# A depthwise convolution on TensorE: eight time phases by sixteen channels in place of four by thirty-two, in a tuned transformer layer

## The chip, the cores and the metric

One Trainium2 chip, all 8 cores. Time is the device time of the slowest core in microseconds (us). The batch has 4 sequences of 4096 tokens; two cores share a sequence. The even cores compute 2176 tokens (two token groups, 1152 and 1024), the odd ones 1920 (768 and 1152) and a halo of 512 tokens of context in front. Nothing is exchanged between cores. In some runs the cores of one die, or of both, show a lower granted clock and the time is 1364 to 1602 us, with most of the kernels here; those runs are set aside and only fast runs are compared. "Even" and "odd" below are the mean span of the four even or odd cores over the fast runs of one kernel.

## The reference, cut to what matters

```python
x = x + 0.5 * swiglu(rmsnorm(x), ...)            # FFN 1
z = rmsnorm(x) @ w_in                            # q, k, v, and u = (a | b) for the convolution
attn_out = chunk_band_attention(q, k, v, bias)   # 8 heads of 64, 576 keys per 64 queries
g  = a * sigmoid(b)                              # GLU, 512 channels
dw = depthwise_causal_conv(g, width=31) + dw_bias
conv_out = silu(layernorm(dw) * ln_g + ln_b)     # norm over the 512 channels
x = x + concat(attn_out, conv_out) @ w_out
x = x + 0.5 * swiglu(rmsnorm(x), ...)            # FFN 2
y = rmsnorm(x)
```

## The kernel before

Each core runs FFN 1, the projections, the convolution, attention, the output projection and FFN 2 on its first token group, and then all of this on the second. From the first down product of FFN 2 of the first group (the matmuls `ps<-at,ring`) to the end of FFN 1 of the second is one long stretch of 393 us, mostly TensorE.

The convolution is done as matmuls. GLU results g[channel, time] go out to DRAM and come back (the "gather") in a phase layout: partition = 32 x phase + channel of the group, column = time / 4. In that layout one matmul against an expanded diagonal matrix of 128 x 128 takes 4 output phases from 4 input phases, and 9 column shifts cover the 31 taps. There are 16 groups of 32 channels:

```python
for s4 in range(4):                         # to_phases(): only after both channel halves are written
    src = d_[:, :, s4, :]
    dst = gp[32 * s4:32 * s4 + 32, :, u0:u0 + W]
    P.dma("sp", ..., reads=(("gs", gi, 0), ("gs", gi, 1)), ...)
...
for grp in range(16):                       # conv()
    for d in range(9):
        mm(b, 0, wv[:, grp % 2, d, :], gp[:, grp, 8 - d:8 - d + U], U, d == 0, d == 8, ...)
    dve(... tensor_scalar(out=acc[:, grp], in0=bank, scalar1=bias, op0=add))     # evacuation
    act(gp[:, grp, 0:U], acc[:, grp], AF.Square, ...)
    if grp > 0:
        pool(... sums += acc[:, grp])
...
for q in range(4):                          # conv_ln(): f32 all the way
    dve(a = a - mean);  dve(a = a * rstd)
for grp in range(16):
    act(co[:, grp, 0:U], acc[:, grp, 0:U], AF.Silu, U, ..., bias=bcol, scale=gcol)
```

U is a quarter of the tokens: 288 and 256 columns on even cores. The kernel places the instructions of all engines in one order by a model of their durations (`P.est`, `P.t`); filler work, the V and Q projections, goes where TensorE would wait by that model. Where the model still expects TensorE to wait for 0.8 us or more, the kernel issues placeholder matmuls (`keep_warm()`, the rows `ps<-cb_sb` of 128x256 at L545), whose results nobody reads. The order is fixed when the kernel is built.

The softmax here doesn't subtract the row's maximum and nothing guards it: scores larger than these inputs give would overflow.

Of the kernel before, what the change touches and what calls it, by code (L numbers as in the profile page):

```python
# [7 lines left out]
F32 = mybir.dt.float32  # L8
# [14 lines left out]
UMAX = MMAX // 4  # L23
GW = UMAX + 8
VW = 520
# [10 lines left out]
CS_LNG = 48  # L36
CS_LNB = 64
CS_RB = 80
CS_N = 84
# [3 lines left out]
CB_I32 = CB_ID + 256  # L43
CB_N = CB_I32 + 32
# [7 lines left out]
RING_COLS = 18832  # L52
# [194 lines left out]
class Group:  # L247


    def __init__(self, gi, blocks):  # L250
# [23 lines left out]
        self.U = self.M // 4  # L274

def build_nc(debug=None):
# [14 lines left out]
    cmp_d = din("cmp", [128, 576])  # L291
# [5 lines left out]
    with ExitStack() as es:  # L297
# [11 lines left out]
        gh_t = sb("gh", 16 * 8 * 2, BF16)[:, :].rearrange("p (g u) -> p g u", g=16)  # L309
# [9 lines left out]
        cmp_t = pb_f[:, 0:576]  # L319
        i32_t = pb_f[:, 576:608]  # L320
# [14 lines left out]
        O_GP = O_ACC + 64 * UMAX  # L335
        O_AB = O_GP + 32 * GW
        O_MV = O_AB + 8 * UMAX
        O_P = O_MV + 8 * UMAX
        O_RS = O_P + 4096
        assert O_RS + 4096 <= D_BYTES  # L340
        O_CV = O_ACC + 32 * UMAX
        qT = carve(O_Q, 8 * MMAX, BF16).rearrange("p (j t) -> p j t", j=4)
        acc = carve(O_ACC, 64 * UMAX, F32).rearrange("p (g u) -> p g u", g=16)
        cvt = carve(O_CV, 8 * MMAX, BF16).rearrange("p (c t) -> p c t", c=4)
        gp = carve(O_GP, 32 * GW, BF16).rearrange("p (g u) -> p g u", g=16)
        co = carve(O_GP, 32 * UMAX, BF16).rearrange("p (g u) -> p g u", g=16)
        sums = carve(O_AB, 4 * UMAX, F32).rearrange("p (i u) -> p i u", i=1)
        mv = carve(O_MV, 8 * UMAX, F32).rearrange("p (i u) -> p i u", i=2)
        mvb = carve(O_MV, 8 * UMAX, BF16).rearrange("p (i u) -> p i u", i=2)
# [18 lines left out]
        cwb = carve(O_GP, 9216, BF16).rearrange("p (i c) -> p i c", i=2)  # L368
# [14 lines left out]
        def make(half):  # L383
# [3 lines left out]
            gs_d = [nc.dram_tensor("gscr%d_%d" % (half, g.gi), [32, 16, 4, g.U + g.hist // 4], BF16).ap() for g in G]  # L387
            cr_d = [nc.dram_tensor("cscr%d_%d" % (half, g.gi), [32, 16, 4, g.U], BF16).ap() for g in G]
            cw_d = nc.dram_tensor("cwscr%d" % half, [8, 128, 2304], BF16).ap()
            gTs = [carve(O_ACC, 32 * (g.U + g.hist // 4), BF16).rearrange("p (c s u) -> p c s u", c=4, s=4) for g in G]  # L390
            c2s = [carve(O_ACC, 32 * g.U, BF16).rearrange("p (c s u) -> p c s u", c=4, s=4) for g in G]
# [39 lines left out]
            for g in G:  # L431
                W = g.U + g.hist // 4
                for c in range(4):
                    P.reg(("g", g.gi, c), "d", O_ACC + c * 8 * W, O_ACC + (c + 1) * 8 * W)
                    P.reg(("c2", g.gi, c), "d", O_ACC + c * 8 * g.U, O_ACC + (c + 1) * 8 * g.U)
            for i in range(16):
# [9 lines left out]
            P.reg("cmp", "pb", 0, 1152)  # L446
            P.reg("i32", "pb", 1152, 1216)
# [14 lines left out]
            P.reg("asum", "d", O_AB, O_AB + 4 * UMAX)  # L462
            P.reg("mean", "d", O_MV, O_MV + 4 * UMAX)
            P.reg("var", "d", O_MV + 4 * UMAX, O_MV + 8 * UMAX)
            P.reg("gph", "d", O_GP, O_GP + 16 * 2 * GW)
            for i in range(2):
                P.reg(("cwb", i), "d", O_GP + 4608 * i, O_GP + 4608 * (i + 1))
# [67 lines left out]
            def keep_warm(gap, skip):  # L535
# [4 lines left out]
                if b is None or P.est("pe", (), (("ps", b),)) > P.t["pe"] + 0.2:  # L540
                    return
                n = int((gap - 0.3) / (0.25 if P.t["pe"] < 9 else 0.125))
                o = bank(b)[:, 0:256]
                for i in range(n):
                    P.op("pe", lambda h: h.matmul(o, lhsT=onesS, rhs=cb[:, B_ONES:B_ONES + 256], start=True, stop=True,  # L545
# [27 lines left out]
            def pool(fn, n, reads, writes):  # L573
                P.op("pool", fn, 0.3 + n / 590.0, reads, writes)
# [457 lines left out]
            def to_phases(g, pc, u0, W):  # L1032
# [9 lines left out]
                if pc == 0:  # L1042
                    return
# [704 lines left out]
```

## Time and profile before

| | us |
|---|---|
| median of 6 runs | 1350.36 |
| even cores, odd cores (mean span, fast runs) | 1347.5 to 1347.9, 1339.4 to 1340.0 |
| core 6, first token group: start to first convolution matmul | 333.9 |
| from there to the first attention matmul | 35.3 |
| from there to the first down product of FFN 2 | 178.2 |
| the rest of FFN 2, and FFN 1 of the second group | 393.2 |
| from there to the first attention matmul of the second group | 75.8 |
| from there to the end | 319.3 |

I cut the run of core 6 into these stages, and asked for the busy time of each engine in each stage. Columns: stage, its length, then the busy time of TensorE (PE), weight loads, VectorE (DVE), ScalarE (ACT) and POOL, then clock, DMA share, GB/s.

```profile
333.90:369.20 35.30, 35.30 (x225) 22.61 (x225) 19.84 (x29) 14.09 (x28) 16.11 (x23) 0.95 0.72 156
369.20:547.40 178.20, 176.12 (x1546) 108.66 (x1546) 76.97 (x160) 89.56 (x149) 34.62 (x35) 1.00 0.40 85
547.40:940.60 393.20, 393.20 (x2075) 202.81 (x2074) 128.40 (x203) 85.47 (x150) 60.30 (x75) 1.00 0.45 85
940.60:1016.40 75.80, 74.20 (x425) 40.98 (x424) 34.97 (x56) 28.88 (x52) 22.72 (x33) 1.00 0.70 160
1016.40:1335.70 319.30, 311.78 (x2223) 168.75 (x2222) 114.93 (x218) 111.47 (x179) 41.32 (x52) 1.00 0.33 64
```

Length less PE busy is PE's idle time: 2.1 us in the first attention stage (which takes in the output projection and the first gate and up products of FFN 2), 7.5 us from the second attention to the end. The elementwise work of the convolution stands in the groups by shape (after the count: busy us, mean ns of one, then the engine's idle time before them and who ended it):

```profile
L1235 DVE TENSOR_SCALAR dreg<-ps,cs_sb 128x288 f32<-128x288 f32 x16 | 8.3, 518 | 14.9 <-PE ps L557 14.2 <-ACT dreg L567 0.7
...
L567 ACT ACTIVATE dreg<-dreg,cs_sb 128x288 bf16<-128x288 f32 x16 | 8.4, 611 | 0.0
L567 ACT ACTIVATE dreg<-dreg 128x512 bf16<-128x512 bf16 x9 | 6.0, 663 | 17.1 <-DVE dreg L1098 17.1
```

In this order: evacuation with the bias, the Silu, and the copy that puts GLU results in phase order. The f32 layernorm (L1277) takes 1358 ns for each of its products.

### The profile page before, as it was taken

Reading aid. Unit: us, or ns where it says so; the run is one execution under the profiler, and the core shown is the slowest. Engines: PE = TensorE matmul, PEld = TensorE weight load, DVE = VectorE, ACT = ScalarE, POOL = GpSimd, SP = SyncE. Lnnn points to the kernel's source line nnn. Section 1 sums busy time; section 2 is a strip of 40 time slices with the busy share of each in tenths; the row PEclk is TensorE's granted clock in tenths of the full one; section 3 lists DMA queues with packets and bytes.
Section 4 is the critical chain, followed back from the end, with each engine's and each line's share of the span. In section 5 each row is a group of like instructions: output and inputs, shape, how many; then the busy total and the mean of one; then the engine's idle time right before and its main releaser. Section 6 shows DMA issues by size and latency. Waiting matters only on the chain.

```text
span 1348.5 us, 22933 instructions; the slowest of 8 cores (1339.4 to 1348.5 us)
## 1 busy us (share of the span) xinstructions
PE 1312.1 (97%) x8454; PEld 736.6 (55%) x8454; DVE 489.0 (36%) x887; ACT 414.2 (31%) x722; POOL 251.6 (19%) x293
## 2 busy tenths in 40 slices
PE   8999999999999999999999999999999999999995
PEld 4565655565666655656555444444466564444444
DVE  4422222362655622222266222225346462122225
ACT  3310011352476531001246110113438661100123
POOL 2360000340402320000062000015140230000012
PEclk9999999999999999999999999999999999999997
DMA  9774226255741473342345744344673016532703
GB/s 220 157 189 80 49 53 115 37 114 132 154 83 23 97 170 63 50 91 51 59 64 104 209 78 85 61 86 85 160 162 85 3 34 124 91 66 45 127 1 127
DMA packets 34882, 127.56 MB, mean 95 GB/s; under 512 B 3408, under 2 KB 13776, under 8 KB 27856
## 3 DMA queue, kind: packets, MB, share of 16 engines
q0 software_dynamic: 18752, 96.10, 38.1%
q1 hardware_dynamic: 16016, 29.95, 7.3%
q8 instruction: 71, 1.16, 0.4%
q14 instruction: 43, 0.35, 0.1%
HBM read 191.98 MB, written 18.09 MB: 156 GB/s over the span
## 4 chain that ended last, share of the span: by engine, by line
PE 90%; DMA 4%; DVE 3%; issue 1%; ACT 1%; POOL 1%; SPq 0%; DVEq 0%; ACTq 0%; POOLq 0%
PE psA L557 52%; PE ps L557 38%; DMA ring<-wgu 2%; DVE hT L813 1%; DMA dreg<-gscr 1%; DMA gscr<-dreg 0%; DMA xres<-xin 0%; ACT rstd L567 0%; POOL xres L700 0%; DVE xres L996 0%; DVE dreg L1412 0%; ACT dreg L567 0%; ACT L565 0%; POOL ring L659 0%; DVE xres L1511 0%
## 5 line engine op out<-in xcount | busy, mean ns | idle before, releaser
L557 PE MATMUL psA<-hT,ring 128*128 128x512 bf16 (+2 forms) x3776 | 700.6, 347 | 5.5 <-DVE hT L813 2.4
L557 PEld LDWEIGHTS psA<-hT,ring 128*128 128x128 bf16 x3776 | 368.0, 98 | 331.7 <-issue 13.5
L567 ACT ACTIVATE dreg<-psA 128x512 f32<-128x512 f32 (+4 forms) x278 | 163.2, 592 | 670.3 <-PE psA L557 662.0
L557 PE MATMUL ps<-at,ring 128*128 128x512 bf16 (+2 forms) x1840 | 326.2, 339 | 0.0
L962 DVE TENSOR_TENSOR at<-psA,dreg 128x512 bf16<-128x512 f32 (+2 forms) x216 | 131.8, 611 | 452.6 <-PE psA L557 435.3
L557 PEld LDWEIGHTS ps<-at,ring 128*128 128x128 bf16 x1840 | 180.0, 98 | 144.4
L996 DVE SCALAR_TENSOR_TENSOR xres<-ps,xres 128x512 f32<-128x512 f32 (+2 forms) x152 | 87.4, 577 | 168.8 <-PE ps L557 168.8
L756 POOL TENSOR_TENSOR ssum<-ssum,sq 128x512 f32<-128x512 f32 (+2 forms) x100 | 104.8, 1049 | 213.2 <-ACT sq L567 210.1
L659 POOL DMA_DIRECT2D ring<-wgu x47 | 28.1, 603 | 476.6 <-PE psA L557 292.5
L557 PE MATMUL ps<-dreg,ring 128*128 128x256 bf16 (+3 forms) x672 | 99.8, 304 | 3.1 <-DMA dreg<-gscr 2.8
L567 ACT ACTIVATE sq<-xres 128x512 bf16<-128x512 f32 (+2 forms) x105 | 55.7, 536 | 105.2 <-DVE xres L996 67.9
L557 PEld LDWEIGHTS ps<-dreg,ring 128*128 128x128 bf16 x672 | 64.3, 99 | 28.6 <-issue 4.9
L813 DVE SCALAR_TENSOR_TENSOR hT<-xres,cs_sb,rstd 128x512 bf16<-128x512 f32 (+2 forms) x112 | 71.6, 696 | 15.0 <-ACT rstd L567 12.4
L557 PE MATMUL ps<-hT,ring 128*128 128x512 bf16 (+2 forms) x320 | 58.9, 339 | 0.0
L565 ACT ACT_TABLE_LOAD x38 | 48.8, 1283 | 0.7
L557 PEld LDWEIGHTS ps<-hT,ring 128*128 128x128 bf16 x320 | 30.9, 98 | 25.1 <-issue 0.2
L567 ACT ACTIVATE dreg<-dreg 128x288 bf16<-128x288 f32 (+6 forms) x53 | 25.4, 479 | 53.4 <-DVE dreg L1235 26.6
L567 ACT ACTIVATE pb<-psA 128x1024 bf16<-128x1024 f32 (+2 forms) x42 | 37.8, 914 | 4.5 <-PE psA L557 4.2
L1511 DVE TENSOR_TENSOR xres<-ps,xres 128x256 f32<-128x256 f32 (+2 forms) x48 | 25.2, 532 | 37.8 <-PE ps L557 37.8
L659 POOL DMA_DIRECT2D ring<-wdA x16 | 8.7, 544 | 131.4 <-PE psA L557 131.4
L1530 POOL TENSOR_TENSOR dreg<-pb 128x2304 bf16<-128x2304 bf16 x8 | 32.3, 4046 | 2.4 <-DMA cwscr<-dreg 2.4
L557 PE MATMUL ps<-at,hT 128*128 128x512 bf16 x136 | 30.7, 379 | 0.0
(89 smaller groups left out, 611.8 us busy)
## 6 DMA issues: line engine op xcount, KB each, us to landing
ring<-wgu POOLq DMA_DIRECT2D x41, 1024.0 KB, 10.0
ring<-wdA POOLq DMA_DIRECT2D x16, 768.0 KB, 8.4
ring<-wdB POOLq DMA_DIRECT2D x16, 640.0 KB, 7.2
ring<-cwscr POOLq DMA_DIRECT2D x16, 576.0 KB, 4.5
cwscr<-dreg SPq DMA_DIRECT2D x8, 576.0 KB, 4.5
ring<-wab POOLq DMA_DIRECT2D x8, 512.0 KB, 7.9
ring<-wout POOLq DMA_DIRECT2D x4, 1024.0 KB, 8.9
dreg<-xin SPq DMA_DIRECT2D x2, 2048.0 KB, 23.4
```

What stands on the lines that cost most here:

```text
L557: P.op("pe", lambda h: h.matmul(o, lhsT=lhsT, rhs=rhs, start=start, stop=stop, skip_group_check=True), (max(n / 2400.0 + 0.0025, 0.03) if ...
L565: P.op("act", lambda h: h.activation(out=cs[0:1, CS_N + i:CS_N + i + 1], in_=onesS[0:1, 0:1], func=func), 1.5, ("cb1",), ())
L567: P.op("act", lambda h: h.activation(out=out, in_=in_, func=func, **kw), 0.12 + n / 1200.0 + (0.09 * sum(isinstance(v, bass.AP) for v in k ...
L659: P.dma("pool", lambda h, dst=dst, src=src: h.dma_start(out=dst, in_=src), wtok(p, i), (256 if p.reads else 512) * w, reads=p.reads, after ...
L756: pool(lambda h: h.tensor_tensor(out=ss, in0=ss, in1=sqt, op=ALU.add), n, (sk, ("sq", i)), (sk,))
L813: dve(lambda h, dst=dst, xin=xin, gcol=gcol: h.scalar_tensor_tensor(out=dst, in0=xin, scalar=gcol, in1=rt, op0=ALU.mult, op1=ALU.mult), n, ...
L962: dve(lambda h: h.tensor_tensor(out=at, in0=ub, in1=tt, op=ALU.mult), n, (("ps", bU), ("tmpF", ti)), (("AT", gi, fl, s),))
L996: dve(lambda h, xo=xo, xi=xi, bk=bk: h.scalar_tensor_tensor(out=xo, in0=bk, scalar=0.5, in1=xi, op0=ALU.mult, op1=ALU.add), n, (("ps", b), ...
L1511: dve(lambda h, xo=xo, bk=bk: h.tensor_tensor(out=xo, in0=bk, in1=xo, op=ALU.add), n, (("ps", b),) + rk, (("x", gi, dm, s),))
L1530: P.op("pool", lambda h, o_=o_, i0=i0: h.tensor_tensor(out=o_, in0=i0, in1=i1, op=ALU.mult), 4.1, ("cmp", "i32", "cb"), (("cwb", i % 2),))
```

## The change

With 8 phases of 16 channels a matmul of half the columns does the same outputs per column, and 5 shifts instead of 9 cover the taps: 32 x 5 = 160 matmuls of an eighth of the tokens in place of 144 of a quarter. Around this the elementwise work is redone: several channel groups share a PSUM bank and are evacuated by one instruction; the gather is split by channel halves, so that the first half can come back while the second is computed; layernorm works in bf16 and takes gain and bias to VectorE; four long Silu replace sixteen. The model's figures for POOL and for the landing of the convolution weights are set higher. The core of the diff, cut:

```diff
-                if pc == 0:
-                    return
-                for s4 in range(4):
-                    src = d_[:, :, s4, :]
-                    dst = gp[32 * s4:32 * s4 + 32, :, u0:u0 + W]
-                    P.dma("sp", ..., reads=(("gs", gi, 0), ("gs", gi, 1)), ...)
-                hold["keys"] = (("gp", 0),)
+                lo, hi = pc * NG // 2, (pc + 1) * NG // 2
+                for s_ in range(PH):
+                    src = gs_d[gi][pc].rearrange("(h j) c s u -> h (j c) s u", h=CH)[:, :, s_, :]
+                    dst = gp[CH * s_:CH * s_ + CH, lo:hi, u0:u0 + W]
+                    P.dma("sp", ..., reads=(("gs", gi, pc),), ...)
+                if pc == 1:
+                    hold["keys"] = (("gp", lo),)
 ...
-                    for d in range(9):
-                        mm(b, 0, wv[:, grp % 2, d, :], gp[:, grp, 8 - d:8 - d + U], U, ...)
+                    for x, grp in enumerate(ids):            # several groups in one bank
+                        for d in range(ND):                  # ND = 5, NG = 32, PH = 8, CH = 16
+                            mm(b, x * U, wv[:, grp % per, d, :], gp[:, grp, HC - d:HC - d + U], U, ...)
+                    dve(... tensor_tensor(out=a3, in0=b3, in1=bc, op=add), m * U)   # one evacuation a bank
 ...
-                    dve(a = a - mean);  dve(a = a * rstd)                           # f32
-                for grp in range(16):
-                    act(co[:, grp], acc[:, grp], AF.Silu, U, bias=bcol, scale=gcol)
+                    dve(c_ = a - mean);  dve(c_ = c_ * rstd)                        # bf16 out
+                    for i in range(nq):                      # 8 groups a quarter, 32 in all
+                        dve(... tensor_scalar(x * gcol + bcol), U)
+                for q, (ck, c_) in enumerate(q_):
+                    act(c_, c_, AF.Silu, nq * U, ck, ck)                            # 4 long ones
 ...
-                P.op("pool", fn, 0.3 + n / 590.0, reads, writes)
+                P.op("pool", fn, 0.45 + n / 490.0, reads, writes)
```

## The prediction

> **What bounds the kernel now.** I read the page first, then the cores, the timeline of TensorE around the convolution, the sub-windows of its granted clock, and the timeline of the queue that issues the transposes.
>
> ```profile
> PE 1312.1 (97%) x8454; PEld 736.6 (55%) x8454; DVE 489.0 (36%) x887; ACT 414.2 (31%) x722; POOL 251.6 (19%) x293
> PE 90%; DMA 4%; DVE 3%; issue 1%; ACT 1%; POOL 1%; SPq 0%; DVEq 0%; ACTq 0%; POOLq 0%
> ```
>
> TensorE (PE) is busy for 97% of the span and is 90% of the chain that ended last. Elementwise time beside it costs nothing; matmul time removed should come off almost whole, and so should PE's waits. The even cores (2176 tokens) set the end at 1347 to 1348.5 us; the odd ones (1920 and a halo) end at 1339 to 1343, so a gain on even cores counts until they meet the odd ones.
>
> Next the convolution, in the timeline of PE: start, length, and in brackets the idle time before it.
>
> ```profile
> 333.88 19.52 PE L557 MATMUL ps<-dreg,ring 128*128 128x288 bf16 x144 [2.79 <-DMA dreg<-gscr]
> ...
> 333.88 6.37 PE L557 MATMUL ps<-dreg,ring 128*128 128x288 bf16 x37 [2.79 <-DMA dreg<-gscr]
> ...
> 988.27 15.94 PE L557 MATMUL ps<-dreg,ring 128*128 128x256 bf16 x144
> ```
>
> A length includes the drain of the last matmul, some 0.17 us. First token group: 144 matmuls of 288 columns. The first 37 took 6.2 us without the drain (168 ns each), the other 107 took 13.15 us (123 ns each). The second group's 144 of 256 columns took 15.8 us (109.6 ns each). The slow start is the clock:
>
> ```profile
> 334.00:337.00 3.00, 3.00 (x15) 1.89 (x14) 0.52 (x1) 0.28 (x1) 1.06 (x2) 0.56 0.36 90
> 337.00:340.00 3.00, 3.00 (x23) 2.27 (x22) 1.03 (x2) 0.81 (x3) 1.30 (x2) 0.87 0.78 303
> 340.00:343.00 3.00, 3.00 (x27) 2.40 (x25) 1.55 (x3) 1.13 (x3) 2.77 (x6) 1.00 0.65 204
> ```
>
> The third column from the right is the granted clock: 0.56 after the wait of 2.79 us, then 0.87, then 1.00. The wait thus cost 2.8 us, and 6.2 - 37 x 0.123 = 1.7 us more. The wait is for the gather of the phase layout out of DRAM; the chain of waits puts the two trips so:
>
> ```profile
> 317.98 5.41 DMA gscr<-dreg
> ...
> 325.64 8.00 DMA dreg<-gscr
> ```
>
> What narrow matmuls cost, each with its own weight load, the timeline of PE in attention shows:
>
> ```profile
> 382.01 0.42 PE L557 MATMUL ps<-at,dreg 128*128 128x65 bf16 x8
> ...
> 385.30 0.39 PE L557 MATMUL ps<-cb_sb,dreg 128*128 128x128 bf16 x4
> ```
>
> Less the last one's modelled length (194 and 218 ns in the groups by shape), seven steps of 65 columns are 0.226 us, 32 ns each, and three of 128 columns 0.172 us, 57 ns each. [...]
>
> [...] The gather of core 5's first group has runs of 400 B (200 positions of bf16) and took 8.5 us from its first issue, at 357.14, to PE's start at 365.65, the 576 B of core 6 took 10.0 us (323.61 to 333.64), and its 512 B in the second group 8.6; no penalty shows down to 400 B, and 288 B no run has shown. [...]
>
> **The change, part by part.** The depthwise convolution is done as matmuls against expanded diagonal matrices. Before: 4 time phases by 32 channels on the partitions, 16 channel groups, 9 shifts. After: 8 phases by 16 channels, 32 groups, 5 shifts; columns per matmul halve.
>
> 1. PE, convolution: group one 144 x 123 ns = 17.7 us becomes 32 x 5 = 160 of 144 columns [...]. Group two 15.8 us becomes 160 of 128 columns at 56 ns (the burst gave 57), 9.0 us: -6.8. Sum -14.5 us.
> 2. PE, statistics: 17 matmuls per group become 32 + 3 and 32 + 4 of half the width; [...]1.9 against 36 x 56 = 2.0. Sum +0.2 us.
> 3. The way to phases. Before, both channel halves must be written before four gathers of 2048 runs start. After, the first half is gathered (8 issues) while the second is computed; PE has about 12 us of gating matmuls between the two first writes (304.6 and 317.0). For the second half: one write (some 5 us), 8 issues at 0.62 us = 5.0 us against 2.6, and half the bytes: my estimate is 0.4 + 4.7 + 5.0 + 3 = 13 us where it was 16.6 (317.0 to 333.6). PE had its last K matmul at about 331.1, which is 14 us after. So the wait of 2.8 and the cold 1.7 us should mostly go: -4.5 us in full, of which I count three quarters, -3.4.
> 4. Convolution weights: pieces of 2560 columns for 2304. Those behind the K weights wait for the gather (as now: POOL issued three from 334.6 to 339.4), then for the first and second pieces to be released. PE now wants a piece each 1.25 us, and the last at 8.8 us after the start; the last can be issued some 3.5 us after the start and takes 4.5 us or more[...]. 0 to 2 us of wait, part of it filled by V projections: +1.
> 5. VectorE. PSUM evacuation: 16 of 518 ns = 8.3 us become 11 of up to 432 columns, at most 0.61 us (from 425 and 692 ns at 256 and 512): 6.5. Layernorm: eight of 1.36 us = 10.8 become four of 1.36 and four bf16 products of about 0.8, and the gain and bias leave ScalarE for 32 small ones of some 0.23 us = 7.5: about 16. Net some +3 us a group.
> 6. ScalarE: 16 Silu of 611 ns = 9.8 us become 4 of about 1.15 = 4.6; Squares 7.1 become about 6. Net -6 us a group. Both engines have slack (53.7 and 40.6 us busy in the 72 us of the first attention), so 5 and 6 matter only where PE waits for them: PE idles 1 us there and 3.1 us in the second. Count 0, with 1.5 us either way.
> 7. The way back: 16 writes of short runs for 8 and 2 large reads for 4: issue 10 us for 5, but it ends long before the output projection, under attention. 0.
> 8. Start: the tap table is 0.65 MB for 0.29 (128 x 1280 f32), but queued behind the first four weight pieces for which PE waits; five memsets go. +0.5.
> 9. The order of instructions is fixed by a model in the program, whose constants for POOL and DMA latency change. PE waits 4.7 us for POOL's sums of squares, mostly in tails without other work. -0.5.
>
> Sum: -14.5 + 0.2 - 3.4 + 1 + 0 + 0.5 - 0.5 = -16.7 on even cores. The order of the whole program shifts, and reordering seldom helps by chance: I give 1 us back, -15.7, so about 1334.7 us. On odd cores the first group has 192 columns (12.1 us for 144)[...]; they would end near 1331 and stay behind the even ones.
>
> **Rivals.**
> A. [...] For: the burst is short and the convolution is a long stream. Against: 32 ns at 65 columns, also in runs of 16. 15%.
> B. The wait for the gather stays or grows: 288 B runs cost as much as 512 B and 8 issues come one after the other. For: each 0.6 us issue is serial. Against: 400 B ran well, and half the work is done early. If it takes 18 us instead of 13, PE idles 4 us and goes cold: about 1340. 20%.
> C. PE becomes bound by DMA on the weights or by VectorE in the layernorm, so that attention starts late: 2 to 6 us lost, 1338 to 1341. Against: PE has V and Q projections to fill with. 20%.
> D. The better-known latencies also remove waits in the attention: 1 to 4 us more, 1331. 15%.
>
> **Range and chances.** 1334.7 us (-1.2%), 8 in 10 between 1329 and 1341. 2% would be 27 us, nearly twice all the matmul time that can go with both waits: faster by over 2% 0.03; slower by over 2% 0.01, as only an unforeseen stall could do it; within 2% 0.96.
>
> **What would show it.** 160 matmuls of 144 and of 128 columns in some 10 and 9 us[...], some 8523 matmuls in all, PE near 1298 us busy; the wait for the gather before the first group under 1 us and the clock at 1.00 behind it (rival B: above 3 us); waits for convolution weights under 2 us (C); VectorE some 6 us up and ScalarE some 12 us down without effect on the span. I am wrong if PE's busy time falls by 14 us and the span does not: then the idle time has moved, most likely to the start of attention.

Where the text is marked as cut, it spoke of the hardware without a trace or run of this case behind it, or rested on that. Three groups of numbers go with the cuts: in step 1 the term of the first group's matmuls, -7.7 us, as the time of a matmul of 144 columns came from there; in step 2 the first group's 0.1; and the odd cores' -5.3 and -7.7. The sum still counts them: -16.7 us on even cores, -15.7 and 1334.7 us with 1 given back, and -13 on odd ones. An estimate of that time from the traces alone, on a straight line between the 57 ns at 128 columns and the 109.6 at 256, is 63.6 ns, so 10.2 us for 160 and a term of -7.5. Rival A, its figures cut, says that narrow matmuls go more slowly in a long stream than in a burst of four. What was cut on the time of a weight load was not shown: the traces record 97 to 99 ns for one, overlapping the next, beside matmuls that follow each other at 32 and 57 ns.

Some other figures are estimates for which the prediction names no trace. An issue was put at 0.62 us, here and in the expectation of run 2; the four gathers of the kernel before took 2.65 us to issue, 0.66 each, and eight of the changed kernel 5.09, 0.64 each. The 0.8 and 0.23 us of step 5 were not measured before the change; afterwards the bf16 product took 752 ns and the 32 small instructions 7.9 us. The 1.15 us of step 6 is near 1.12, a straight line through ScalarE's 595 ns at 512 columns and 1016 at 1024. And "elementwise time beside it costs nothing" was an assumption.

## The result and the profile after

The changed kernel takes 1334.65 us (median of the timed runs; the fast ones go from 1332.5 to 1338.1). The ratio to the kernel before, which is the mean time of one kernel's fast runs over that of the other's of the same rounds and so not quite the ratio of the medians, is 0.9882 (95% interval 0.9871 to 0.9894): 1.2% less, within the 2% that counts as the same. The predicted time was 1334.7.

The sum is right. The question is therefore whether its terms are. First the spans, in the view by core of the profiled run: core 2, the slowest, takes 1331.4 us, core 5 1330.0 and core 6 1329.4, at clocks of 0.995 and 0.996.

Before, core 5 took 1343.4 and core 6 1348.5. Even cores gained some 18 us, odd ones 10, and now they tie. The prediction had odd cores near 1331 and "behind the even ones": they are at 1330.1, but the even ones came down to 1329.7 as well. With eight cores so close the slowest of a run is whichever had a bad moment (1338.1 in one run was odd core 3 alone at 1336.5), and 2 of the 18 us are lost in that maximum: the even cores gained 18, the slowest core 16.

The page has the busy times, the chain that ended last and the packets:

```profile
PE 1291.7 (97%) x8399; PEld 727.1 (55%) x8511; DVE 499.2 (37%) x938; ACT 400.9 (30%) x673; POOL 250.5 (19%) x281
...
DMA packets 42433, 129.39 MB, mean 97 GB/s; under 512 B 20048, under 2 KB 22224, under 8 KB 35408
...
PE 93%; DVE 3%; issue 2%; ACT 1%; DMA 0%; DVEq 0%; ACTq 0%
```

DMA has gone from 4% of the chain to nothing and small packets rose from 3408 to 20048. (Here 112 matmul records are missing against the 8511 weight loads, where the kernel before has 8454 of each, so busy PE is a little low.) The timeline of PE in the two convolutions of core 6:

```profile
330.10 6.45 PE L567 MATMUL ps<-dreg,ring 128*128 128x144 bf16 x100
336.38 1.89 PE L567 MATMUL ps<-at,hT 128*128 128x512 bf16 x8
338.15 1.10 PE L567 MATMUL ps<-dreg,ring 128*128 128x144 bf16 x15
...
340.81 2.99 PE L567 MATMUL ps<-dreg,ring 128*128 128x144 bf16 x45
...
975.90 5.78 PE L567 MATMUL ps<-dreg,ring 128*128 128x128 bf16 x100
```

No bracket stands behind the first line: there is no wait for the gather. A hundred matmuls of 144 columns took 6.45 - 0.17 = 6.28 us, 62.8 ns each (0.17 is the drain of the last: one lasts 226 ns in the groups by shape, 0.16 us more than the step); a hundred of 128 took 5.61, 56 ns each. The eight matmuls of 512 columns in between are V projections, put there by the kernel's model because it expects the next weight piece late.

The same stages as before, core 6:

```profile
330.10:356.30 26.20, 26.20 (x263) 18.37 (x262) 13.18 (x24) 10.18 (x20) 15.19 (x19) 1.00 0.90 199
356.30:538.20 181.90, 176.65 (x1547) 108.33 (x1547) 90.17 (x197) 84.22 (x132) 32.87 (x35) 1.00 0.41 87
538.20:931.40 393.20, 393.20 (x2075) 202.81 (x2073) 126.92 (x202) 85.59 (x150) 61.07 (x75) 1.00 0.44 85
931.40:1000.80 69.40, 67.50 (x458) 36.14 (x455) 31.16 (x51) 27.95 (x42) 20.88 (x25) 1.00 0.72 174
1000.80:1316.50 315.70, 310.48 (x2210) 168.05 (x2210) 122.06 (x249) 105.51 (x165) 41.66 (x52) 1.00 0.34 66
```

Read it against the first table. The convolution starts 3.8 us earlier and its stage is 9.1 us shorter, as hoped or better. But the first attention stage is 3.7 us longer, with the same 1546 or 1547 matmuls and the same busy PE: its idle time went from 2.1 to 5.2 us. And the last stage is 3.6 us shorter, though the prediction expected 0.5 there.

The waits of PE over the whole run (waited for, us in total, times, longest):

```profile
PE ps L567 <- DVE dreg L1443: 2.5, 5, 0.7
PE ps L567 <- DVE xres L1542: 2.2, 3, 1.0
...
PE ps L567 <- DVE dreg L1026: 1.7, 1, 1.7
PE ps L567 <- POOL ssb L771: 1.6, 1, 1.6
```

The same view cut to the first attention stage gives VectorE most of the idle time there: the output projection's residual (L1542) holds PE for all of its 2.2 us, the evacuation L1026 for its 1.7, attention's normalisation (L1443) for 0.4. Before, none of the three held PE in that stage. The other 2.1 us of L1443 (1.6 before) and the wait for POOL's sums, which fell from 4.7 to 1.6, are elsewhere.

The last stage is shorter for a reason that this list hides. In PE's timeline of the kernel before, between the second output projection (it ends at 1105.4) and FFN 2:

```profile
1105.45 1.04 PE L545 MATMUL ps<-cb_sb 128*128 128x256 bf16 x8
1107.84 0.40 PE L557 MATMUL ps<-ssb,cb_sb 128*128 128x256 bf16 x2 [1.35 <-POOL ssb L761]
...
1108.19 1.91 PE L545 MATMUL ps<-cb_sb 128*128 128x256 bf16 x16
1110.43 4.91 PE L557 MATMUL psA<-hT,ring 128*128 128x512 bf16 x22 [0.33 <-DVE hT L813]
```

For 5.0 us PE has three small statistics matmuls and 24 placeholders: it waits for POOL's sums and what is computed from them. This gap is 5.0 to 5.2 us on all four even cores. In the changed kernel it is 0.2 us or less on all four, as matmuls of the output projection and of FFN 2 stand around the statistics:

```profile
1079.51 4.73 PE L567 MATMUL ps<-dreg,ring 128*128 128x256 bf16 x40
1084.07 3.62 PE L567 MATMUL psA<-hT,ring 128*128 128x512 bf16 x16
```

In return 16 placeholders (1.9 us) stand in the second attention of core 6.

And the elementwise groups:

```profile
L1251 DVE TENSOR_TENSOR dreg<-ps,cs_sb 128x432 f32<-128x432 f32 x10 | 6.1, 608 | 4.4 <-PE ps L567 4.4
L1300 DVE TENSOR_TENSOR dreg<-dreg 128x1152 bf16<-128x1152 f32 x4 | 5.4, 1353 | 0.0
L1303 DVE TENSOR_TENSOR dreg<-dreg 128x1152 bf16<-128x1152 bf16 x4 | 3.0, 752 | 0.2 <-DVE dreg L1300 0.2
L1309 DVE TENSOR_SCALAR dreg<-dreg,cs_sb 128x144 bf16<-128x144 bf16 x32 | 7.9, 314 | 0.4
...
L577 ACT ACTIVATE dreg<-dreg 128x512 bf16<-128x512 bf16 x9 | 10.1, 1120 | 15.9 <-DVE dreg L1103 15.9
L577 ACT ACTIVATE dreg<-dreg 128x1152 bf16<-128x1152 bf16 x4 | 4.4, 1150 | 2.1 <-DVE dreg L1309 2.1
```

VectorE's layernorm takes 5.4 + 3.0 + 7.9 = 16.3 us a group (predicted: about 16), the four Silu 4.4 (4.6). One row was not predicted: the same copy into phase order on ScalarE takes 1120 ns in place of 663. It now reads every eighth element of a row and writes eight pieces for four; which of the two costs the time is not shown.

### The profile page after: what moved, and what is told of

It reads as the page before. It is cut to its first block, busy times and chain, and to the rows that moved or that the text cites. A ratio compares the mean times of both kernels' runs of the same rounds, so it can differ in the third digit from the quotient of the medians.

```text
span 1331.4 us, 22938 instructions; the slowest of 8 cores (1327.5 to 1331.4 us)
## 1 busy us (share of the span) xinstructions
PE 1291.7 (97%) x8399; PEld 727.1 (55%) x8511; DVE 499.2 (37%) x938; ACT 400.9 (30%) x673; POOL 250.5 (19%) x281
## 2 busy tenths in 40 slices
DMA packets 42433, 129.39 MB, mean 97 GB/s; under 512 B 20048, under 2 KB 22224, under 8 KB 35408
## 4 chain that ended last, share of the span: by engine, by line
PE 93%; DVE 3%; issue 2%; ACT 1%; DMA 0%; DVEq 0%; ACTq 0%
PE psA L567 54%; PE ps L567 39%; DVE hT L823 1%; PE ps L555 1%; DVE xres L823 0%; DMA xres<-xin 0%; DVE xres L1006 0%; DVE dreg L1443 0%; ACT pb L577 0%; ACT L575 0%; DVE xres L1542 0%; ACT rstd L577 0%; ACT dreg L577 0%; DVE dreg L1439 0%; ACT L577 0%
## 5 line engine op out<-in xcount | busy, mean ns | idle before, releaser
L567 PEld LDWEIGHTS psA<-hT,ring 128*128 128x128 bf16 x3760 | 367.0, 98 | 329.2 <-issue 12.9
L577 ACT ACTIVATE sq<-xres 128x512 bf16<-128x512 f32 (+2 forms) x105 | 55.5, 536 | 107.9 <-DVE xres L1006 66.8
L567 PE MATMUL ps<-dreg,ring 128*128 128x256 bf16 (+4 forms) x694 | 81.5, 272 | 2.6 <-DVE xres L1542 1.4
L823 DVE SCALAR_TENSOR_TENSOR hT<-xres,cs_sb,rstd 128x512 bf16<-128x512 f32 (+2 forms) x112 | 74.4, 721 | 11.9 <-ACT rstd L577 9.7
L567 PEld LDWEIGHTS ps<-dreg,ring 128*128 128x128 bf16 x704 | 55.2, 98 | 22.5 <-issue 4.1
L567 PE MATMUL ps<-hT,ring 128*128 128x512 bf16 (+2 forms) x331 | 61.7, 340 | 0.3
L577 ACT ACTIVATE dreg<-dreg 128x432 bf16<-128x432 f32 (+11 forms) x48 | 36.7, 778 | 44.9 <-DVE dreg L1103 23.1
L1562 POOL TENSOR_TENSOR dreg<-pb 128x2560 bf16<-128x2560 bf16 x8 | 35.8, 4498 | 5.6 <-DVE cb_sb L1583 5.5
L1542 DVE TENSOR_TENSOR xres<-ps,xres 128x256 f32<-128x256 f32 (+2 forms) x48 | 24.6, 530 | 24.6 <-PE ps L567 23.7
```

The costliest lines, as they stand in the source:

```text
L567: P.op("pe", lambda h: h.matmul(o, lhsT=lhsT, rhs=rhs, start=start, stop=stop, skip_group_check=True), (max(n / 2400.0 + 0.0025, 0.03) if ...
L577: P.op("act", lambda h: h.activation(out=out, in_=in_, func=func, **kw), 0.12 + n / 1200.0 + (0.09 * sum(isinstance(v, bass.AP) for v in k ...
L823: dve(lambda h, dst=dst, xin=xin, gcol=gcol: h.scalar_tensor_tensor(out=dst, in0=xin, scalar=gcol, in1=rt, op0=ALU.mult, op1=ALU.mult), n, ...
L1542: dve(lambda h, xo=xo, bk=bk: h.tensor_tensor(out=xo, in0=bk, in1=xo, op=ALU.add), n, (("ps", b),) + rk, (("x", gi, dm, s),))
L1562: P.op("pool", lambda h, o_=o_, i0=i0: h.tensor_tensor(out=o_, in0=i0, in1=i1, op=ALU.mult), 4.5, ("cmp", "ic", "cb"), (("cwb", i % 2),))
```

## The experiments

Twelve runs, each with five timed rounds. "Even" and "odd" are means over fast runs; the kernel before, in the same batches, has 1347.5 to 1347.9 and 1339.4 to 1340.0.

| run | mean us | ratio to before (95%) | even | odd |
|---|---|---|---|---|
| changed kernel | 1334.5 | 0.9882 (0.9871 to 0.9894) | 1329.7 | 1330.1 |
| 1 halves gathered early, in before | 1346.2 | 0.9965 (0.9952 to 0.9979) | 1343.1 | 1338.2 |
| 2 gather late, in the changed one | 1349.8 | 0.9992 (0.9979 to 1.0005) | 1345.3 | 1336.6 |
| 3 convolution matmuls twice | 1343.9 | 0.9948 (0.9935 to 0.9961) | 1341.0 | 1339.7 |
| 4 POOL figure alone, in before | 1349.8 | 0.9992 (0.9979 to 1.0005) | 1346.6 | 1339.5 |
| 5 gain and bias on ScalarE | 1343.2 | 0.9943 (0.9930 to 0.9957) | 1333.9 | 1340.2 |
| 6 weights not held | 1333.0 | 0.9865 (0.9847 to 0.9883) | 1328.9 | 1327.4 |
| 7 old figures of the model | 1337.1 | 0.9895 (0.9877 to 0.9913) | 1328.9 | 1334.1 |
| 8 gain and bias on POOL | 1338.5 | 0.9905 (0.9890 to 0.9920) | 1329.8 | 1335.0 |
| 9 half the columns, in before | 1344.0 | 0.9953 (0.9938 to 0.9967) | 1338.9 | 1330.3 |
| 10 half the columns and halves early, in before | 1336.4 | 0.9898 (0.9880 to 0.9917) | 1333.7 | 1329.2 |
| 11 not held, Silu placed later | 1335.2 | 0.9889 (0.9873 to 0.9905) | 1332.2 | 1329.0 |
| 12 changed kernel again | 1334.9 | 0.9893 (0.9874 to 0.9912) | 1329.7 | 1329.5 |

Runs 1 to 4, 5 to 8 and 9 to 12 were three batches, each with its own runs of the kernel before on the same chip; the even cores of before differ by 0.4 us between batches. The first line, the changed kernel's own result, was taken apart from these, so run 12 repeats it.

### 1. The kernel before, with the gather by channel halves

```diff
-                if pc == 0:
-                    return
+                lo, hi = 8 * pc, 8 * pc + 8
                 for s4 in range(4):
-                    src = d_[:, :, s4, :]
-                    dst = gp[32 * s4:32 * s4 + 32, :, u0:u0 + W]
+                    src = d_[:, lo:hi, s4, :]
+                    dst = gp[32 * s4:32 * s4 + 32, lo:hi, u0:u0 + W]
-                          ... reads=(("gs", gi, 0), ("gs", gi, 1)), ...
+                          ... reads=(("gs", gi, pc),), ...
```

> The kernel before (4 phases) with only the gather split: the first channel half is gathered as soon as it is written. Theory (the wait of 2.8 us for the gather plus 1.7 us of cold clock is a part of the gain by itself): on the even cores PE's wait for the gather ahead of the first group's convolution is under 0.5 us and the clock is at 1.00 behind it, the even cores end 4 to 4.5 us earlier (about 1343 for 1347.5), the odd ones (0.4 to 2 us of such waits) 0 to 2 us earlier, time about 1346. Rival (the wait only moves, for example to the weights of the convolution, or the early gather collides with the second half's writes): the time is within 1 us of before.

The even cores gained 4.7 us, the odd ones 1.8. In PE's timeline the convolution stands without a wait, 3.0 us earlier, and at a granted clock of 1.00 from its start (144 matmuls in 17.86 - 0.17 us are 123 ns each):

```profile
330.84 17.86 PE L557 MATMUL ps<-dreg,ring 128*128 128x288 bf16 x144
```

So the gain is about the 4.5 us that the prediction gave the wait and the cold clock "in full", and gathering halves early brings it without any of the new layout. That the two figures agree is in part luck: in the profile of the kernel before all four even cores wait (2.5 to 2.8 us), but only cores 0 and 6 start slowly (19.52 us for the 144 matmuls; 17.85 on cores 2 and 4). Wait and cold clock come to some 3.5 us on the mean even core; where the rest of the 4.7 lies was not looked into.

### 2. The changed kernel, with all gathers after both writes

```diff
+                if pc == 0:
+                    return
+                for q in range(2):
+                    ... 8 gathers of half q, reads=(("gs", gi, 0), ("gs", gi, 1)) ...
```

> The changed kernel with its early gather undone: all 16 gathers are issued once both halves are written. Theory (early start pays for the doubled number of gathers): the gathers now need 16 issues of 0.62 us = 10 us and land some 5 us later, about 5 us after PE's last K matmul. If the order doesn't adapt, the even cores end 5 to 7 us later (wait plus cold clock). Rival (PE has enough other work, V and Q projections, and the order is made by a model that knows of the 16 issues): wait under 1 us and the even cores within 1.5 us of the changed kernel.

Both theories missed: the even cores lost 15.6 us, three times what run 1 had gained. PE hardly waits at the convolution (0.73 us for the gather and 0.75 for a weight piece), because V projections are put in its place. Most of the loss comes afterwards:

```profile
358.40:549.20 190.80, 183.58 (x1594) 114.25 (x1594) 90.50 (x198) 85.61 (x137) 32.23 (x35) 0.99 0.41 87
```

The first attention stage lasts 190.8 us for 181.9. PE is idle in 7.2 of them, and 5.6 us more are 48 placeholders, of which the changed kernel has none there. (The start of the convolution is 2.1 us later, the second group's stage before attention 2.4 longer, the last 3.2.) In a short stretch of it ScalarE is full (after the length the figures are PE, weight loads, DVE, ACT), and PE's 47 matmuls are mostly placeholders:

```profile
390.00:396.00 6.00, 5.25 (x47) 4.32 (x46) 1.26 (x5) 5.97 (x8) 0.00 (x0) 1.00 0.32 50
...
390.96 4.86 PE L555 MATMUL ps<-cb_sb 128*128 128x256 bf16 x43
```

With the filler spent earlier, PE follows the exps of ScalarE, and at 414 us it waits 2.2 us for attention's normalisation on VectorE. A transfer that seems hidden by filler has used up that filler: its cost is seen where the filler would have been needed. That the filler is the reason is my reading; the place of the loss is measured.

### 3. The changed kernel, every convolution matmul twice

```diff
-                        for d in range(ND):
+                        for d in [i for i in range(ND) for r in range(2)]:
```

The sums double before the bias; layernorm takes a common factor out. The outputs are right.

> The changed kernel with every convolution matmul done twice (wrong result on purpose: the sums double before the bias). Theory (convolution time on PE counts one for one): even cores +160 x 62.5 ns + 160 x 56 ns = +19 us, odd cores +6.8 + 10 = +17 us, time about 1353. Rival (the convolution is partly hidden behind gather, weights or evacuation, so the removed matmul time is not what came off): +10 us or less.

It costs 11.3 us on even cores and 9.6 on odd ones, for 160 x 62.8 ns + 160 x 56 ns = 19.0 us of matmuls on even cores, at the times measured in the changed kernel (here 207 of 144 columns in one piece took 13.18 - 0.17 us, 62.9 each): 0.6 of it. By stages on core 6: the first convolution starts 1.9 later and its stage is 10.0 longer, the second's is 8.7 longer, as they should be; but the first attention stage is 176.9 in place of 181.9, and the last stage 2.3 us shorter.

```profile
368.20:545.10 176.90, 174.67 (x1546) 108.84 (x1546) 82.96 (x180) 82.90 (x131) 32.40 (x35) 1.00 0.41 86
```

PE's idle time there is 2.2 us, as it was in the kernel before, without placeholders in either. A longer convolution is partly paid back by an attention with fewer waits.

### 4. The kernel before, with the new figure for POOL

```diff
-                P.op("pool", fn, 0.3 + n / 590.0, reads, writes)
+                P.op("pool", fn, 0.45 + n / 490.0, reads, writes)
```

> The kernel before with only the two constants by which the program estimates an instruction of POOL when it fixes the order (0.45 + n/490 for 0.3 + n/590 us). Nothing that runs is removed or added except by the order. My sum gave this part -0.5 us; the comparison of the traces shows PE's waits for POOL's sums of squares down from 4.7 to 1.6 us. Theory A (the better estimate removed these waits): waits for the sums under 2 us and even cores 2 to 3 us earlier. Theory B (they fell because the shorter convolution shifted the order): waits as before, time within 1 us.

The wait for POOL's sums fell from 4.7 to 1.8 us, and the time hardly followed: 1.1 us on even cores, the ratio 0.9992 with 1 in the interval. Other waits grew (hT from 2.4 to 3.4, the attention's normalisation from 1.6 to 2.7), and much of this one was filled and not removed: the gap before FFN 2 of the second group is still 4.6 us on core 6, with 29 placeholders in it for 24.

### 5. The changed kernel, gain and bias on ScalarE

```diff
-                    for i in range(nq):
-                        dve(... tensor_scalar(out=x, in0=x, scalar1=gcol, scalar2=bcol, op0=mult, op1=add), U)
-                for q, (ck, c_) in enumerate(q_):
-                    act(c_, c_, AF.Silu, nq * U, ck, ck)
+                for grp in range(NG):
+                    act(co[:, grp, 0:U], co[:, grp, 0:U], AF.Silu, U, ..., bias=bcol, scale=gcol)
```

> The changed kernel with the gain and bias of the layernorm put back into the Silu of ScalarE (32 Silu of 144 columns with two per-partition operands, some 0.5 us each, for 32 small VectorE instructions and 4 long Silu). My prediction gave the shift between the engines 0 on the time. The trace of the changed kernel shows VectorE busy 5.0 to 5.6 of each 6 us from 354 to 381 us, and ScalarE's last Silu waiting 2.1 us for it while PE idles 1.8 us and its fillers run out. Theory 1 (VectorE in the layernorm delays the attention behind it): the even cores gain 1 to 4 us. Theory 2 (either engine's block stands in the way of the exponentials alike): within 1.5 us, or up to 4 us worse as ScalarE has 11 us more per group.

It is 4.2 us slower on even cores and 10 on odd ones. It is not an exact undo: the 32 Silu take 12.8 us of ScalarE in the first group (one lasts 491 ns), where the kernel before had 16 in 8.4 and the changed one has 4 in 4.4. So it shows that moving this work matters, and in which direction, more than how much the change gained by it. Where it is lost on core 6, against the changed kernel:

```profile
1004.80:1323.70 318.90, 311.14 (x2203) 169.87 (x2231) 115.66 (x220) 115.49 (x195) 41.43 (x52) 1.00 0.35 66
```

The last stage is 3.2 us longer, 318.9, nearly the 319.3 of the kernel before; the first attention stage 0.9 (182.8). It is not the loss that the kernel before has: the gap before FFN 2 stays closed (0.2 us). Here 33 placeholders (3.8 us, for 16 in 1.9) stand in the second attention at 1022.7, while ScalarE does the 32 Silu in one piece of 12.4 us (the four long ones: 3.9), with exps of attention behind them. On core 5 it was 6.2 us in the first attention stage (133.5 for 127.3) and 4.1 from the second attention to the end.

### 6. The changed kernel, convolution weights not held back for the gather

```diff
-                              reads=p.reads, after=hold["keys"], ...
+                              reads=p.reads, after=() if p.reads else hold["keys"], ...
```

> The changed kernel, but the convolution's weight pieces are no longer held back until the gather has landed. In the changed kernel three of eight pieces are issued only at the start of the convolution, so the order puts 24 V matmuls of 512 columns (5.2 us) between its banks on the even cores, and on the odd cores PE waits 2.3 to 3.3 us for a piece besides. Theory (late weights spend filler work that PE then lacks in the attention): convolution in one piece or nearly, waits for weights under 0.5 us, odd cores 2 to 4 us earlier (1327), even cores 1 to 4 us earlier. Rival (the weights collide with the gather, which lands later by as much): wait for the gather 1 to 3 us, time within 1.5 us of the changed kernel.

Odd cores gained 2.7 us: in the changed kernel cores 1, 3 and 5 wait 2.3, 2.3 and 3.3 us for a piece of the convolution weights, and here none does. Even cores, which have V projections to put there, gained 0.8. This version has the lowest time of all, 1333.0; its interval overlaps that of the changed kernel (0.9847 to 0.9883 and 0.9871 to 0.9894), so that it is faster on the whole is likely but not shown.

### 7. The changed kernel with the old figures of the model

```diff
-                P.op("pool", fn, 0.45 + n / 490.0, reads, writes)
+                P.op("pool", fn, 0.3 + n / 590.0, reads, writes)
-                              ..., issue=0.55, late=3.5 if p.reads else 2.0)
+                              ..., issue=0.55)
```

> The changed kernel with the old constants of the order's model (POOL 0.3 + n/590, landing of convolution weights 2.0 us for 3.5). Theory (the constants matter only as the order happens to fall; the kernel before with the new POOL constants gained 0.5 us): within 2 us of the changed kernel on the even cores, with V matmuls no longer between the convolution's banks and a wait of 1 to 3 us for weights in their place. Rival (the new constants are worth several us in this kernel): 3 to 6 us slower.

Even cores 0.8 us less, odd ones 4 more. For the even cores the new figures are worth nothing; the odd ones need them in the new layout.

### 8. The changed kernel, gain and bias on POOL

```diff
-                        dve(lambda h, ...: h.tensor_scalar(out=x, in0=x, scalar1=gcol, ...), U, ...)
-                        if i == nq // 2 - 1:
-                            yield lambda: P.t["dve"] - 1.0
+                        pool(lambda h, ...: h.tensor_scalar(out=x, in0=x, scalar1=gcol, ...), U, ...)
```

> The changed kernel with the 32 small gain-and-bias instructions of each group on POOL, which is idle from 352 to 396 us, for VectorE. Theory 1 (VectorE's 8 us in the layernorm delay the first attention): VectorE is busy 8 us less per group in the attention, Silu comes earlier, the even cores gain 1 to 4 us. Rival (POOL is slower, over 0.5 us an instruction, so that the Silu and with it the output projection come later): even cores 0 to 5 us later.

Even cores the same (1329.8), odd ones 5 us more. In the first attention stage POOL is busy for 51.7 us with 67 instructions, in the changed kernel for 32.9 with 35: the 32 more come to 0.59 us each, where VectorE needed 7.9 us for all. The last stage of core 6 is 314.8 us, as short as with VectorE. So for the even cores it matters that ScalarE does not have this work (run 5), and not which other engine does.

### 9. The kernel before, eight of nine matmuls with half the columns

```diff
+                        Ud = U if d == 0 else U // 2
-                        mm(b, 0, wv[:, grp % 2, d, :], gp[:, grp, 8 - d:8 - d + U], U, ...)
+                        mm(b, 0, wv[:, grp % 2, d, :], gp[:, grp, 8 - d:8 - d + Ud], Ud, ...)
```

The result is wrong (relative error 0.32).

> The kernel before, with eight of the nine matmuls of each channel group shortened to half their columns (the first keeps its width, so that all of the bank is written; the values are wrong on purpose). It removes matmul time from the convolution and touches nothing else: 128 x (123 - 62.5) ns = 7.7 us and 128 x (109.6 - 56) ns = 6.9 us on even cores, 14.6 in sum, by chance what step 1 of the prediction removes; on odd cores 128 x (82.5 - 42.5) = 5.1 and 6.9, 12.0. Theory 1 (matmul time taken from the convolution comes off the span one for one, as step 1 counts it): the even cores end 14 to 15 us earlier than before, the odd ones 11.5 to 12.5, the span near 1336. Theory 2 (it comes off at some 0.6, as the matmuls done twice cost only 11.3 of 19, the rest being hidden under waits of the convolution for evacuation, sums or weights): even cores 8 to 10 us earlier. The wait for the gather stays at 2.8 us under both.

The matmul times in the expectation are close to what the traces show: 123 and 82.8 ns for 288 and 192 columns, 62.8 and 42.7 for 144 and 96 (core 5 of the changed kernel: 60 in 2.73 - 0.17 us). Even cores gained 8.6 us, odd ones 9.1: theory 2 on the even cores, in between on the odd ones (9.1 of 12.0). In PE's timeline the convolution itself shrank as planned, behind the old wait:

```profile
333.72 10.61 PE L557 MATMUL ps<-dreg,ring 128*128 128x288 bf16 x144 [2.51 <-DMA dreg<-gscr]
```

By stages: -8.9 in the first convolution and -5.0 in the second, but +3.0 in the first attention stage (idle time 4.3 for 2.1 us). The rival's reason was wrong on core 6: waits inside the convolution are not what eats the gain there; it is eaten afterwards, as in run 3. Elsewhere the rival has a part: PE waits 1.6 us on core 2 and 1.4 to 2.3 on the odd cores for weights of the convolution, for which it does not wait in the kernel before. One disturbance: on core 6 the granted clock stayed at 1.00 after the wait of 2.51 us (0.56 in the kernel before, after 2.79), so some of its 8.9 is cold clock that the kernel before had. The 8.6 us are a mean over the four even cores and the fast runs.

### 10. The kernel before, both parts: half the columns and halves gathered early

The edits of runs 1 and 9 together; wrong again.

> The kernel before with both parts that the prediction credits: the gather by channel halves (alone it gave 4.7 us on even cores and 1.2 to 1.8 on odd ones) and the shortened matmuls of the run just before (values wrong on purpose). Nothing of the new elementwise work, constants or piece sizes is in it. Theory 1 (the parts add up): the even cores gain the sum of the two single runs within 1.5 us, and if that sum is near 18 the two parts carry the whole gain of the changed kernel on even cores. Theory 2 (they overlap, because with half the matmul time the convolution is bound by evacuation, the POOL sums or the weights, and the earlier start only lets PE wait for these): at least 3 us less than the sum. Odd cores: the sum of the single runs, some 13, under theory 1, so that they end near 1327 and stay behind the even ones; the changed kernel's odd ones gained only 10 to 11.7.

Even cores gained 13.8 us; the sum of the single runs is 13.3. The parts add up, but to 14 and not to 18. Odd cores gained 10.2 and not 13; the changed kernel has 9.3 to 9.9 on them. The stages of core 6:

```profile
330.00:356.40 26.40, 26.14 (x227) 17.41 (x225) 14.68 (x26) 12.15 (x26) 16.07 (x23) 1.00 0.90 194
356.40:537.40 181.00, 176.76 (x1546) 109.42 (x1546) 86.10 (x167) 87.43 (x143) 32.29 (x35) 1.00 0.40 86
...
1001.60:1320.50 318.90, 311.53 (x2223) 168.64 (x2222) 117.72 (x219) 111.99 (x180) 41.38 (x52) 1.00 0.32 64
```

Up to FFN 2 these are the changed kernel's figures within a microsecond (26.4 and 181.0 for 26.2 and 181.9), although layernorm, Silu, evacuation, model figures and weight pieces are the old ones. So the 3 us that come back in the first attention belong to the shorter convolution, not to VectorE's longer layernorm; runs 5 and 8, which take 8 us from VectorE in that stage, agree (182.8 and 182.4). The last stage, however, is that of the kernel before: 318.9 for 319.3, where the changed kernel has 315.7. The gap before FFN 2 is in it, 4.6 to 4.9 us on the even cores.

### 11. An attempt at a better version

Run 6, with the Silu placed in ScalarE's order for later:

```diff
-                yield lambda: max(P.est("act", (("co", NG - 1),)) - 3.5, P.t["act"] - 1.0)
+                yield lambda: max(P.est("act", (("co", NG - 1),)) - 1.0, P.t["act"] - 1.0)
```

> The changed kernel with the convolution weights not held for the gather (as in the earlier run, 1333.0 us as a mean) and the four long Silu placed in ScalarE's order for 1 us before the gains and biases are done instead of 3.5: an attempt to beat both kernels. ScalarE waited 2.1 us for VectorE at the first Silu, with the exps of attention behind it, and PE had only 4.5 of 6 us of work in that stretch. Theory 1 (that stall costs PE time that is not won back): 1 to 2 us less than the not-held kernel, 1331 to 1332. Theory 2 (the order of the rest shifts with it, and the convolution's way back ends later): no gain, within 1 us either way or slower.

Theory 2, and worse than it said: even cores 3.3 us more than in run 6. The first attention stage of core 6 lasts 184.6 us for 181.3, with 20 placeholders (2.5 us) for none. A stall of 2.1 us that is plain to see on ScalarE was worth keeping.

### 12. The changed kernel again

> The changed kernel once more, unaltered, on the same chip as the two candidates and parts above, so that they can be set beside it without a change of chip. Both theories: 1333.5 to 1336 us, even cores 17.5 to 18.5 us earlier than before, odd cores 10 to 12.

1329.7 on even and 1329.5 on odd cores, 17.8 and 9.9 less than before on the same chip: as expected, but for the odd ones, 0.1 below the range.

## Why the prediction was right, and where it was not

The terms of the sum, by stages of core 6. The middle column puts the prediction's own steps in the stages where they belong, step 4 halved between the groups; the measured columns are single profiles, in which the start of the convolution alone varies by about 1.4 us between two runs of the changed kernel (330.1 and 328.7).

| stage | predicted (steps) | changed less before | run 10 less before |
|---|---|---|---|
| start to first attention matmul | -7.7 + 0.1 - 3.4 + 0.5 + 0.5 = -10.0 (1, 2, 3, 4, 8) | -12.9 | -12.8 |
| first attention to FFN 2's first down product | 0 (5, 6, 7) | +3.7 | +2.8 |
| rest of FFN 2, FFN 1 | 0 | 0.0 | +0.1 |
| second group up to attention | -6.8 + 0.1 + 0.5 = -6.2 (1, 2, 4) | -6.4 | -4.9 |
| second attention to the end | -0.5 (9) | -3.6 | -0.4 |
| sum | -16.7 | -19.2 | -15.2 |
| even cores, mean of fast runs | -16.7, less 1 given back | -17.8 | -13.8 |

Point by point:

- **Matmul durations (step 1), right.** 10.0 and 9.0 us were predicted for the two convolutions. The pieces in PE's timeline give 6.28 + 0.93 + 2.82 = 10.0 and 5.61 + 2.24 + 1.12 = 9.0. Streams of a hundred, each matmul with its own weight load, ran at 62.8 ns for 144 columns and 56 for 128, no slower than the burst of four (57): rival A is refuted.
- **What they are worth (step 1), wrong.** "Matmul time removed should come off almost whole" is the step that failed. Adding 19.0 us of matmuls cost 11.3 (run 3), removing 14.6 gave 8.6 (run 9), on top of the early gather 9.2 (run 10 less run 1): 0.6 each time on even cores (odd ones: 0.6 to 0.8). PE busy in 97% of the span was no proof, and the placeholders are part of the 97%. The prediction named the sign of this itself: the idle time has moved, most likely to the start of attention. PE's idle time in the first attention stage more than doubles (2.1 to 5.2 us). Why is my reading and not shown: the order of five engines is fixed, and a shorter convolution makes attention start while ScalarE and VectorE, which attention needs too, still have the convolution's normalisation to do.
- **The wait and the cold clock (step 3), right in mechanism and a little low.** 3.4 was counted; alone it gave 4.7 (run 1), on top of the narrow matmuls 5.2 (run 10 less run 9). The write and gather of the second half took from 316.25 to 330.1 at most, 13.9 us; 13 was my estimate. The cold 1.7 us was read on core 6 and counted for all even cores; in the same profile cores 2 and 4 do not have it. The length of the wait alone did not decide: waits of 2.79 us (core 6) and 2.47 us (core 0) led to granted clocks of 0.56 and 0.61 in the 3 us from 334, waits of 2.72 (core 2) and 2.58 (core 4) to 1.00. Rival B is refuted: the runs of 288 B cost no wait. The packets under 512 B rose from 3408 to 20048, the eight issues of a half took 5.09 us; what such a gather costs by itself no run here measured.
- **Weights (step 4), right for the even cores, left out for the odd ones.** 0.8 us on even cores (1 was counted), where V projections fill in, 2.7 on odd ones (run 6), for which the prediction counted nothing; there rival C, a wait for weights of over 2 us, came true.
- **VectorE and ScalarE (steps 5 and 6): durations right, worth wrong.** +5.5 us for layernorm and -1.7 for evacuation on VectorE in the first group, -4.0 for Silu on ScalarE; but "count 0" missed some 4 us on even cores, which is what the changed kernel has beyond run 10. The traces show where: the gap before FFN 2 of the second group is 4.6 to 5.2 us on every even core of every version with the old elementwise work (before, runs 1, 4, 9 and 10), and 0.2 or less with the new (changed kernel, runs 2, 3, 5 to 8 and 11). What closes it is not isolated: not the engine of gain and bias (runs 5 and 8) nor the model's figures (runs 4 and 7); the order of PE's work around it differs.
- **A false lead.** It looks as if ScalarE's busy time in the last stage set its length: 111.5 us before, 112.0 in run 10 and 115.5 in run 5 go with 319 us, 105.5 in the changed kernel and 105.8 in run 8 with 315, but run 3, with 107.9, took 313.4, and run 2, with 107.4, took 318.9; and the 318.9 of run 10 has the gap, that of run 5 placeholders behind the Silu.
- **The same part on odd cores.** It seems worth nothing beside run 10 (10.2), but without the wait for weights (run 6) they gain 12.0, so that some 2 us may be hidden; that run 5 costs them 10 stays open.
- **A cost left out.** The copy into phase order takes 1120 ns for 663 on ScalarE, 6.4 us more over the nine long and eight shorter ones (busy 9.9 before, 16.3 after). Why a copy with every eighth element takes longer than one with every fourth is not shown. The copy lies where ScalarE has time, and no run isolates what it costs the span.
- **The model's figures (step 9), wrong in its reason.** The wait for POOL's sums did fall, from 4.7 to 1.6 us, and the gap before FFN 2 went with it, but the new figures did not do it: in run 4 they left the gap at 4.6 us and gave even cores 1.1, in run 7 the old ones were back, the gap stayed closed and the even cores lost nothing. That the better figures would remove waits in attention (rival D) is refuted by the same two runs.
- **Odd cores.** Predicted -13, measured -9.3 to -9.9, with the weights' wait of 2 to 3 us as the part that run 6 shows. They now set the end as often as the even ones, which the prediction excluded.

So 1334.7 came out of errors that cancel, which is luck. On even cores the prediction's -16.7 is -14.5 (step 1), -3.4 (step 3) and +1.2 for all the rest. The runs give -8.6 (run 9), -5.2 (run 10 less run 9) and -4.0 (the changed kernel less run 10), in sum -17.8; and 2 us of this go in the tie of the cores, where 1 had been set aside.

## What to carry to other kernels

When a part of a busy engine's work is cut, ask what other engines must do in the time that it covered: here each microsecond of matmuls before attention was worth 0.6 on the even cores, in both directions, at 97% busy. Ask also what the busy time is made of: placeholders made waits look like work, and a gap of 5 us showed in the list of waits as 1.35 of POOL and 0.33 of VectorE. Look for a gain at the stage after the one changed, by cutting both traces at the same instructions and comparing length and idle time stage by stage; the total alone hid two shifts of nearly 4 us each. And check the two halves of a change alone in the old kernel: the early gather by halves needed none of the new layout.
